# Mixer B's sample values on Trainium2: from two 64-column matmuls of 256 moving columns to four 32-column matmuls of 128

## The chip, the cores and the metric

The kernel runs on one core of a Trainium2 chip. The metric is the device time of one execution in microseconds (us), the median of several runs.

## What is computed

One step of a hybrid decoder layer over 1024 prompt rows and a group of 8 samples with 8 new tokens each. A projection of the inputs feeds two attention mixers, whose gated outputs go through a branch projection and an output projection with a layer norm. All data are float32. What the change touches is the attention of mixer B for the samples, over the cached keys and values of three head groups (window and dilation 128/1, 512/4, 2048/16); cut to that:

```python
def _gathered_attention(q, k, v, start, q_pos, dists, sink):
    ...
    s = jnp.einsum('nthgd,ntjhd->nthgj', q, kg).astype(jnp.float32) * SCALE
    p, lse = _masked_softmax(s, valid[None, :, None, None, :], sink)
    o = jnp.einsum('nthgj,ntjhd->nthgd', p.astype(v.dtype), vg)
    return o, lse
...
    for (win, dil), cache, q, k, v in zip(B_PAIRS, caches_b, qb, kb, vb):
        ...
        o, lse = _gathered_attention(q, kv[:, :, 0], kv[:, :, 1], PAST_LEN - cb, q_pos,
                                     np.arange(0, win + 1, dil), None)
        ...
    ob = _combine_dilations(outs, lses)
```

There are 4 key/value heads of 64 channels, 2 query heads to each, 8 samples and 8 new tokens.

## The kernel before

**The whole.** `in_proj` multiplies the weights by all rows, split into a high and a low part so that each product is three matmuls (L170, L171, L172, in chunks of 384, 384 and 320 moving columns). Weights come by DMA on the SP queue (`wraw<-w_in`), are rounded on ACT (`whi`, L89) and subtracted on DVE (`wlo`, L90). In its second part, `in_proj` makes the gates, and a generator, `beside()`, is advanced by a tick after every group of products: first the prompt's attention, then the samples' mixer A (`decode_a`), then the samples' mixer B (`decode_b`), then `merge`, which weighs and gates the attention outputs. Each tick lets the generator issue its next few instructions, so the program order on each engine is fixed when the kernel is built. Then come the branch projection (L1015 to L1017) and the output projection (L1058 to L1060).

**`decode_b`.** The samples go in four quads of two samples (`j` = 0, 1). For a quad, seven steps make the scores (L688, and L692 for the new keys), a softmax follows, and seven value steps add up the products of probabilities and values. Each of the 14 steps of a quad reads one tile `kv` (three buffers; loaded on POOL's queue two steps ahead, L661 for keys, L663 for values). 128 score rows stand on the partitions: 64 per sample, of which 32 belong to one pair of key/value heads (`kp` = 0, 1).

**A value step.** `transposes(gi + 1)` turns the probabilities of the next step (L726, copied to `pt` by ACT, L730). Then for each of the step's blocks of 128 keys (one in the first step, two in the other six) there are two matmuls (L746), one per sample: 64 columns of `pt` are the stationary operand, in half of the array's columns (`tile_position=(0, 64 * j)`), and 256 columns of `v`, all four heads, are the moving one. The first step adds the new tokens' values in the same way, with 24 rows (L741). All accumulate in one PSUM tile `acc` [128, 256].

**After the value steps.** DVE scales `acc` by the softmax's denominator (L751, into `o`), two steps of the generator later two transposes turn `o` (L756), and four copies on ACT (L762) take out, for each `kp`, the rows of `kp` in the columns of `kp`:

```python
pr = pa[:, :256].rearrange("d (k b q h g t) -> d k q h g b t", k=2, b=2, q=2, h=2, g=2)
...
        nc.scalar.copy(sr[r, kp, :, 2 * quad:2 * quad + 2], pr[r, kp, kp, h2])
```

The other half of `acc`, rows of one `kp` against columns of the other, is not read.

Of the kernel before, what the change touches and what calls it, by code (L numbers as in the profile page):

```python
# [10 lines left out]
F32 = mybir.dt.float32  # L11
# [3 lines left out]
ALU = mybir.AluOpType  # L15
# [4 lines left out]
P = 128  # L20
# [85 lines left out]
def layer_kernel(ctx: ExitStack, tc: tile.TileContext, A, O, S):  # L106
    nc = tc.nc
# [4 lines left out]
    ident = const.tile([P, P], F32, tag="ident", name="ident")  # L112
# [4 lines left out]
    def psd():  # L117
        return ps.tile([P, 512], F32, tag="d", name="psd")

    def psa():  # L120
        return ps.tile([P, 512], F32, tag="a", name="psa")
# [518 lines left out]
    def decode_b():  # L640
        with tc.tile_pool(name="db", bufs=1, side="right", reuse_waits="tile") as dp:
# [10 lines left out]
            def get(q, i):  # L652
                n = todo.index((q, i))
                for q_, i_ in todo[n:n + 3]:
                    if (q_, i_) not in tiles:
                        t = dp.tile([P, 2, 2, 256], F32, tag="kv", name="kv", bufs=3)
                        j, w = i_ % 7, COLS[i_ % 7]
                        for h in range(2):
                            if i_ < 7:
                                c = sum(COLS[:j])  # L660
                                nc.gpsimd.dma_start(out=t[:, h, :, :w], in_=A["ktb"][2 * q_ + h, :, :, c:c + w])  # L661
                            else:
                                nc.gpsimd.dma_start(out=t[:, h, :w // P], in_=A["vb"][2 * q_ + h, :, 2 * j - (j > 0):2 * j + 1])  # L663
                        tiles[q_, i_] = t
                return tiles[q, i]
# [4 lines left out]
            for quad in range(NB // 2):  # L670
                bs = (2 * quad, 2 * quad + 1)
                s = dp.tile([P, 1688], F32, tag="s", name="s")
                st = dp.tile([P, 16], F32, tag="st", name="st", bufs=2)
                vnew = dp.tile([24, 2, 256], F32, tag="vnew", name="vnew", bufs=1)
                for g in range(3):
                    for i in range(2):
                        nc.gpsimd.dma_start(
                            out=vnew[NQ * g:NQ * (g + 1), :, P * i:P * (i + 1)],
                            in_=S["sv"][1 + 2 * g + i, 16 * quad:16 * (quad + 1)].rearrange("(b t) c -> t b c", b=2))

                for ci in range(7):
                    cols, g = COLS[ci], (0, 1, 1, 2, 2, 2, 2)[ci]
                    pa = psa()
                    k = get(quad, ci)
                    for j, b in enumerate(bs):
                        for kp in range(2):
                            r = 64 * j + 32 * kp
                            nc.tensor.matmul(pa[r:r + 32, :cols], lhsT=qbd[:, g, b, kp], rhs=k[:, j, kp, :cols],  # L688
                                             start=True, stop=True, tile_position=(0, r))
                            if ci == 0:  # L690
                                for gg in range(3):
                                    nc.tensor.matmul(  # L692
                                        pa[r:r + 32, 128 + 8 * gg:136 + 8 * gg], lhsT=qbd[:, gg, b, kp],
                                        rhs=knew[:, gg, kp, NQ * b:NQ * (b + 1)], start=True, stop=True,
                                        tile_position=(0, r))
                    if ci == 0:
                        mm, sv, pv = mk[:, :152], s[:, :152], pa[:, :152]
                    elif g == 1:
                        lo = 152 + 256 * (ci - 1)
                        mm, sv, pv = mk[:, lo:lo + 256], s[:, lo:lo + 256], pa[:, :256]  # L700
                    else:
                        lo = 664 + 256 * (ci - 3)
                        mm = mk[:, 664 + 2 * (ci - 3):666 + 2 * (ci - 3)].unsqueeze(2).to_broadcast([P, 2, P])
                        sv = s[:, lo:lo + 256].rearrange("p (c k) -> p c k", c=2)
                        pv = pa[:, :256].rearrange("p (c k) -> p c k", c=2)
                    nc.vector.tensor_tensor(out=sv, in0=pv, in1=mm, op=ALU.add)
                    yield
                nc.vector.tensor_reduce(out=st[:, 0:1], in_=s, axis=AX.X, op=ALU.max)
                nc.vector.tensor_scalar(out=st[:, 1:2], in0=st[:, 0:1], scalar1=-0.125, scalar2=None, op0=ALU.mult)
                nc.scalar.activation(s, s, AF.Exp, bias=st[:, 1:2], scale=0.125, accum_out=st[:, 2:3])  # L710
                nc.vector.reciprocal(out=st[:, 3:4], in_=st[:, 2:3])
                yield
                yield
                yield
                acc = psa()
                starts = [0] + [152 + 128 * i for i in range(12)]
                ptn = dp.tile([24, P], F32, tag="ptn", name="ptn")
                ps_ = []

                def transposes(gi):  # L720
                    pa = psa()
                    p = dp.tile([P, 2, P], F32, tag="pt", name="pt", bufs=2)
                    w = COLS[gi] // P
                    for j in range(w):
                        c = starts[2 * gi - (gi > 0) + j]
                        nc.tensor.transpose(pa[:, P * j:P * (j + 1)], s[:, c:c + P], ident)  # L726
                    if gi == 0:
                        nc.tensor.transpose(pa[:24, P:2 * P], s[:, 128:152], ident)
                        nc.scalar.copy(ptn, pa[:24, P:2 * P])
                    nc.scalar.copy(p[:, :w], pa[:, :P * w].rearrange("p (b k) -> p b k", k=P))  # L730
                    ps_.append(p)

                transposes(0)
                yield
                for gi in range(7):
                    if gi < 6:
                        transposes(gi + 1)
                    p = ps_.pop(0)
                    if gi == 0:
                        for j in range(2):  # L740
                            nc.tensor.matmul(acc[64 * j:64 * (j + 1), :256], lhsT=ptn[:, 64 * j:64 * (j + 1)],  # L741
                                             rhs=vnew[:, j], start=True, stop=False, tile_position=(0, 64 * j))
                    v = get(quad, 7 + gi)
                    for jb in range(COLS[gi] // P):
                        for j in range(2):
                            nc.tensor.matmul(  # L746
                                acc[64 * j:64 * (j + 1), :256], lhsT=p[:, jb, 64 * j:64 * (j + 1)],
                                rhs=v[:, j, jb], start=False, stop=(gi == 6 and jb == 1), tile_position=(0, 64 * j))
                    yield
                o = dp.tile([P, 256], F32, tag="o", name="o")  # L750
                nc.vector.tensor_scalar(out=o, in0=acc[:, :256], scalar1=st[:, 3:4], scalar2=None, op0=ALU.mult)  # L751
                yield
                yield
                pa = psa()
                for kp in range(2):
                    nc.tensor.transpose(pa[:, P * kp:P * (kp + 1)], o[:, P * kp:P * (kp + 1)], ident)  # L756
                pr = pa[:, :256].rearrange("d (k b q h g t) -> d k q h g b t", k=2, b=2, q=2, h=2, g=2)
                sr = so.rearrange("d k g (b t) -> d k g b t", b=NB)
                for kp in range(2):
                    for h2 in range(2):  # L760
                        r = slice(HD * h2, HD * (h2 + 1))
                        nc.scalar.copy(sr[r, kp, :, 2 * quad:2 * quad + 2], pr[r, kp, kp, h2])  # L762
            for kp in range(2):
                for h2 in range(2):
                    nc.gpsimd.dma_start(out=S["num"][8 + 2 * kp + h2, :, NT:].rearrange("(g d) t -> d g t", g=2),
# [231 lines left out]
    gi = 78 * 4  # L997
    for part, (a, b) in enumerate(CHUNKS):
# [4 lines left out]
        for ft in range(KT):  # L1003
            ga, gb = nxt
            pa, pb = psd()[:, :n], psa()[:, :n]
            for j in range(3):
# [3 lines left out]
                o = pa if j < 2 else pb  # L1010
                for k4 in range(4):
                    k = 4 * j + k4
                    h, l = whi[:, k4 * P:(k4 + 1) * P], wlo[:, k4 * P:(k4 + 1) * P]
                    st, en = k in (0, 8), k in (7, 11)
# [19 lines left out]
        for i, (t, c) in enumerate(tiles):  # L1034
            h = hp.tile([P, DM], F32, tag=f"h{i}", name=f"h{i}")
# [43 lines left out]
        for nq in range(4):  # L1079
            pt = [psd() if i < 2 else psa() for i in range(len(tiles))]  # L1080
            if last and nq == 3:
                ws = []
                for i, (t, c) in enumerate(tiles):
# [8 lines left out]
                    h = hs[i][:c]  # L1092
                    v = mv[:c, 4 * i:4 * i + 4]
# [18 lines left out]
        if not last:  # L1112
            after(2, lambda: nc.scalar.activation(m4[:, :, 2], m4[:, :, 1], AF.Sqrt, bias=epst))
            nxt = load_g(0, *CHUNKS[part + 1])
            for i, (t, c) in enumerate(tiles):
                h, v = hs[i], mv[:, 4 * i:4 * i + 4]
# [133 lines left out]
```

## Time and profile before

| | |
|---|---|
| median of 3 runs | 2870.86 us (2870.16 to 2871.94) |
| the profiled execution's own time | 2865.24 us |
| its span, first to last instruction | 2863.5 us |
| PE (TensorE matmul) busy | 2760.6 us, 96% |
| DVE (VectorE) busy | 1530.0 us, 53% |
| ACT (ScalarE) busy | 925.8 us, 32% |
| POOL (GpSimd) busy | 770.9 us, 27% |
| mean granted TensorE clock | 0.983 of full speed |

PEld is TensorE's loading of the stationary operand. A float32 matmul instruction shows as two records (a high and a low pass), each with its own weight load; the text calls one record a pass. Matmul ends are modelled and overlap the next start, so the text takes times from one start to a later start. "Idle before" is an engine's idle time ahead of an instruction, with what ended it. The profiled execution is 5.6 us shorter than the median of the runs.

### The profile page before, as it was taken

The page shows a single profiled execution, that of the slowest core. Times are in us where ns is not written, and L with a number is a line of the kernel's source. Part 1 is how long each engine was busy: PE and PEld are TensorE (multiplying, and loading weights), DVE is VectorE, ACT ScalarE, POOL GpSimd, SP SyncE. Part 2 cuts the span into 40 slices and gives each one's busy share as a digit, 9 for nine tenths or more (in the row PEclk, how much of TensorE's full clock was granted, in tenths as well). Part 3 has the DMA queues.
Part 4 walks back from the last instruction along what each step waited for, and adds up shares of the span by engine and source line. Part 5 has one row for each costly group of instructions (what it writes and reads, how often), then busy time and mean ns, then how long its engine had stood idle before and what let it go on. Part 6 is the DMA issues. An engine that isn't in the chain of part 4 may idle for free.

```text
span 2863.5 us, 42950 instructions
## 1 busy us (share of the span) xinstructions
PE 2760.6 (96%) x16423; PEld 2641.7 (92%) x16423; DVE 1530.0 (53%) x2600; ACT 925.8 (32%) x1857; POOL 770.9 (27%) x589
## 2 busy tenths in 40 slices
PE   8999999999989999999999999999999996997898
PEld 8999999989989999999999998889899886986886
DVE  5444433423426778777665422116556458557856
ACT  4222222222223544444443321223144323432442
POOL 0000000000005666677677613432100025004201
PEclk9999999999999999999999999999999997998899
DMA  6345564465463333455445445559866535643662
GB/s 217 101 126 164 165 187 150 156 190 167 142 198 110 116 111 114 136 153 150 142 144 149 123 119 189 182 168 284 276 202 233 188 120 168 241 131 105 205 220 96
DMA packets 224965, 467.60 MB, mean 163 GB/s; under 512 B 33896, under 2 KB 151208, under 8 KB 221240
## 3 DMA queue, kind: packets, MB, share of 16 engines
q1 hardware_dynamic: 206264, 405.09, 45.0%
q0 software_dynamic: 16400, 52.43, 6.1%
q10 hardware_dynamic: 2096, 7.34, 0.7%
q8 instruction: 129, 2.11, 0.3%
q14 instruction: 76, 0.62, 0.1%
HBM read 365.17 MB, written 144.21 MB: 178 GB/s over the span
## 4 chain that ended last, share of the span: by engine, by line
PE 84%; DVE 6%; DMA 5%; SPq 2%; issue 1%; ACT 1%; POOL 0%; ACTq 0%; DVEq 0%; POOLq 0%
PE psd L170 19%; PE psd L172 18%; PE psd L171 18%; PE psd L1060 3%; PE psd L1059 3%; PE psd L1058 3%; PE psa L425 2%; PE psd L1017 2%; PE psd L1016 2%; PE psd L1015 2%; DMA wraw<-w_in 2%; DVE wlo L90 2%; SPq L321 1%; PE psa L487 1%; PE psa L486 1%
## 5 line engine op out<-in xcount | busy, mean ns | idle before, releaser
L170 PE MATMUL psd<-xhi,whi 128*128 128x384 f32 (+1 forms) x3712 | 1226.2, 330 | 26.4 <-ACT whi L89 23.8
L172 PE MATMUL psd<-xhi,wlo 128*128 128x384 f32 (+1 forms) x3712 | 1219.5, 329 | 2.1 <-DVE wlo L90 1.7
L171 PE MATMUL psd<-xlo,whi 128*128 128x384 f32 (+1 forms) x3712 | 1217.8, 328 | 0.3 <-DVE xlo L226 0.3
L90 DVE TENSOR_TENSOR wlo<-wraw,whi 128x512 fp32r<-128x512 f32 x648 | 482.2, 766 | 653.6 <-ACT whi L89 641.7
L170 PEld LDWEIGHTS psd<-xhi,whi 128*128 128x128 f32 x3712 | 699.9, 189 | 48.9 <-ACT whi L89 26.3
L172 PEld LDWEIGHTS psd<-xhi,wlo 128*128 128x128 f32 x3712 | 699.3, 188 | 5.7 <-DVE wlo L90 5.7
L171 PEld LDWEIGHTS psd<-xlo,whi 128*128 128x128 f32 x3712 | 699.7, 189 | 0.8 <-DVE xlo L226 0.8
L89 ACT CAST whi<-wraw 128x512 fp32r<-128x512 f32 x648 | 385.7, 618 | 592.2 <-DMA wraw<-w_in 348.8
L446 POOL PARTITION_ALL_REDUCE md<-s x160 | 214.6, 1341 | 1038.9 <-DMA vst<-s_vs 865.0
L460 POOL PARTITION_ALL_REDUCE md<-s x160 | 310.0, 1938 | 67.4 <-ACT s L457 44.2
L477 DVE TENSOR_TENSOR pl<-s,ph 128x512 fp32r<-128x512 f32 (+1 forms) x160 | 127.9, 800 | 100.4 <-ACT ph L476 98.4
L1017 PE MATMUL psd<-y,wlo 128*128 128x384 f32 (+1 forms) x384 | 129.1, 336 | 29.7 <-DVE wlo L90 29.7
L985 POOL TENSOR_TENSOR h<-h,mv 128x2048 f32<-128x2048 f32 x6 | 21.6, 3608 | 484.1 <-ACT whi L89 276.3
L1015 PE MATMUL psd<-y,whi 128*128 128x384 f32 (+1 forms) x384 | 129.1, 336 | 21.6 <-ACT whi L89 21.6
L1060 PE MATMUL psd<-wlo,m 128*128 128x512 f32 x384 | 149.8, 390 | 0.0
L1059 PE MATMUL psd<-whi,m 128*128 128x512 f32 x384 | 149.7, 390 | 0.0
L1058 PE MATMUL psd<-whi,m 128*128 128x512 f32 x384 | 149.6, 390 | 0.0
L457 ACT ACTIVATE s<-s 128x256 f32<-128x256 f32 (+1 forms) x160 | 75.9, 475 | 195.9 <-DVE s L456 193.8
L951 ACT ACTIVATE z<-psd,bias 128x384 f32<-128x384 f32 x132 | 73.8, 562 | 195.1 <-PE psd L172 129.4
L1016 PE MATMUL psd<-y,whi 128*128 128x384 f32 (+1 forms) x384 | 128.3, 334 | 0.0
L491 DVE TENSOR_TENSOR num<-psa,pvl 64x256 f32<-64x256 f32 x160 | 66.1, 413 | 77.3 <-ACT pvl L490 76.6
L1017 PEld LDWEIGHTS psd<-y,wlo 128*128 128x128 f32 x384 | 74.4, 194 | 32.1 <-DVE wlo L90 32.1
(202 smaller groups left out, 3183.4 us busy)
## 6 DMA issues: line engine op xcount, KB each, us to landing
wraw<-w_in SPq DMA_DIRECT2D x152, 512.0 KB
wraw<-w_out SPq DMA_DIRECT2D x96, 512.0 KB
wraw<-w_br SPq DMA_DIRECT2D x72, 512.0 KB
o_c<-c SPq DMA_DIRECT2D x64, 510.0 KB
qst<-s_qs SPq DMA_DIRECT2D x80, 256.0 KB
s_zg<-z SPq DMA_DIRECT2D x64, 192.0 KB
kv<-ktb POOLq DMA_DIRECT2D x48, 256.0 KB, 3.4
kv<-vb POOLq DMA_DIRECT2D x48, 256.0 KB, 3.1
```

The source lines that it names most:

```text
L89: self.nc.scalar.copy(hi, raw)
L90: self.nc.vector.tensor_tensor(out=lo, in0=raw, in1=hi.bitcast(F32), op=ALU.subtract)
L170: nc.tensor.matmul(o, lhsT=h, rhs=xhi[k][:, a:b], start=(k == 0), stop=False)
L171: nc.tensor.matmul(o, lhsT=h, rhs=xlo[k][:, a:b], start=False, stop=False)
L172: nc.tensor.matmul(o, lhsT=l, rhs=xhi[k][:, a:b], start=False, stop=(k == KT - 1))
L446: nc.gpsimd.partition_all_reduce(u["md"][:, 0], top, P, RED.max)
L460: nc.gpsimd.partition_all_reduce(u["md"][:, 1], s[:, 1 if n == 1 else 2], P, RED.add)
L1015: nc.tensor.matmul(o, lhsT=h, rhs=yt[k][:, 0, :n], start=st, stop=False)
L1017: nc.tensor.matmul(o, lhsT=l, rhs=yt[k][:, 0, :n], start=False, stop=en)
L1058: nc.tensor.matmul(pt, lhsT=h, rhs=whi, start=st, stop=False)
L1059: nc.tensor.matmul(pt, lhsT=l, rhs=whi, start=False, stop=False)
L1060: nc.tensor.matmul(pt, lhsT=h, rhs=wlo, start=False, stop=en)
```

## The change

The same products are made in quarters. For each block of 128 keys there are four matmuls in place of two, one per sample `j` and head pair `kp`: 32 columns of `pt` at array column `r = 64 * j + 32 * kp`, and only the 128 columns of `v` that belong to that `kp`. The new tokens' values go the same way. `acc` is used to 128 columns, `o` becomes [128, 128], one transpose takes the place of two, and the four copies read the smaller tile.

```diff
+                    ROWS = [(j, kp, 64 * j + 32 * kp) for j in range(2) for kp in range(2)]
                     if gi == 0:
-                        for j in range(2):
-                            nc.tensor.matmul(acc[64 * j:64 * (j + 1), :256], lhsT=ptn[:, 64 * j:64 * (j + 1)],
-                                             rhs=vnew[:, j], start=True, stop=False, tile_position=(0, 64 * j))
+                        for j, kp, r in ROWS:
+                            nc.tensor.matmul(acc[r:r + 32, :P], lhsT=ptn[:, r:r + 32],
+                                             rhs=vnew[:, j, P * kp:P * (kp + 1)], start=True, stop=False,
+                                             tile_position=(0, r))
                     v = get(quad, 7 + gi)
                     for jb in range(COLS[gi] // P):
-                        for j in range(2):
+                        for j, kp, r in ROWS:
                             nc.tensor.matmul(
-                                acc[64 * j:64 * (j + 1), :256], lhsT=p[:, jb, 64 * j:64 * (j + 1)],
-                                rhs=v[:, j, jb], start=False, stop=(gi == 6 and jb == 1), tile_position=(0, 64 * j))
+                                acc[r:r + 32, :P], lhsT=p[:, jb, r:r + 32],
+                                rhs=v[:, j, jb, P * kp:P * (kp + 1)], start=False, stop=(gi == 6 and jb == 1),
+                                tile_position=(0, r))
                     yield
-                o = dp.tile([P, 256], F32, tag="o", name="o")
-                nc.vector.tensor_scalar(out=o, in0=acc[:, :256], scalar1=st[:, 3:4], scalar2=None, op0=ALU.mult)
+                o = dp.tile([P, P], F32, tag="o", name="o")
+                nc.vector.tensor_scalar(out=o, in0=acc[:, :P], scalar1=st[:, 3:4], scalar2=None, op0=ALU.mult)
                 yield
                 yield
                 pa = psa()
-                for kp in range(2):
-                    nc.tensor.transpose(pa[:, P * kp:P * (kp + 1)], o[:, P * kp:P * (kp + 1)], ident)
-                pr = pa[:, :256].rearrange("d (k b q h g t) -> d k q h g b t", k=2, b=2, q=2, h=2, g=2)
+                nc.tensor.transpose(pa[:, :P], o, ident)
+                pr = pa[:, :P].rearrange("d (b q h g t) -> d q h g b t", b=2, q=2, h=2, g=2)
```

On PE, this is the difference of the two programs at the fourth and fifth value steps of the first quad, which stand directly behind each other (`s` are the probabilities, `ident` the identity of the transposes, `xhi_` and `xlo_` the parts of the layer's input):

```order
 L172 MATMUL psd<-xhi_155,wlo 128x384
 L726 MATMUL psa<-ident,s 128x128 x2
-L746 MATMUL psa<-kv,pt 64x256 x4
+L749 MATMUL psa<-kv,pt 32x128 x8
 L726 MATMUL psa<-ident,s 128x128 x2
-L746 MATMUL psa<-kv,pt 64x256 x4
+L749 MATMUL psa<-kv,pt 32x128 x8
 L170 MATMUL psd<-xhi_126,whi 128x384
```

The matmuls stand where they stood, twice as many, each of half the moving columns and half the array columns.

On POOL, this stands at the passage from `decode_b` to `merge`, with what each row waits for, before (`so` is the quad's output, `w`, `z` and `m` are merge's first tiles):

```order
471 L765 DMA s_num<-so 64x2x64 [waits DMASW3_49,Activation_49]
472 L841 DMA w<-s_wa 64x1024 [waits DMASW7_49,DMASW6_49,DMAHW2_49,DMASW4_49,PE_49]
473 L841 DMA w<-s_wa 64x1024 [waits DMASW5_49]
474 L844 DMA z<-s_z 128x1088 [waits DVE_49]
475 L798 DMA m<-s_md 32x1x256 [waits DVE_49,PE_49]
```

and this in the changed program:

```order
471 L768 DMA s_num<-so 64x2x64 [waits DMASW3_49,Activation_49]
472 L844 DMA w<-s_wa 64x1024 [waits DMASW5_49,DMAHW2_49,DMASW4_49,PE_49]
473 L844 DMA w<-s_wa 64x1024
474 L847 DMA z<-s_z 128x1088 [waits DMASW6_49,DMASW7_49,DVE_49,PE_49]
475 L801 DMA m<-s_md 32x1x256 [waits PE_49]
```

The order is the same; since `o` is smaller, merge's tiles lie over other tiles of `decode_b`, and the waits on its loads and on PE have moved between neighbouring rows.

## Rows read from the trace of the kernel before

**Rows 1.** The page: busy time, and the chain that ended last by engine.

```profile
PE 2760.6 (96%) x16423; PEld 2641.7 (92%) x16423; DVE 1530.0 (53%) x2600; ACT 925.8 (32%) x1857; POOL 770.9 (27%) x589
...
PE 84%; DVE 6%; DMA 5%; SPq 2%; issue 1%; ACT 1%; POOL 0%; ACTq 0%; DVEq 0%; POOLq 0%
```

**Rows 2.** Busy time by stretch: us, engines (instructions), granted clock, DMA share, GB/s.

```profile
1740.00:1760.00 20.00, 20.00 (x132) 15.12 (x129) 2.47 (x4) 3.04 (x8) 9.38 (x16) 1.00 0.65 205
1900.00:1920.00 20.00, 20.00 (x129) 17.05 (x128) 2.56 (x4) 5.17 (x13) 4.16 (x8) 1.00 0.26 84
1920.00:2080.00 160.00, 153.33 (x916) 152.21 (x916) 91.44 (x106) 41.22 (x68) 39.49 (x74) 0.99 0.91 280
```

**Rows 3.** Line L746: durations (ns min/median/max), first and last start (us), waits.

```profile
L746 PE MATMUL psa<-kv,pt x208: 378/379/432, 1740.2 to 1910.5; 128*64 128x256 f32 x104
...
  issue: 4.2, 24
  ACT pt L730: 1.2, 3
```

**Rows 4.** PE in order of time, a quad's first value steps: start, us, instruction, passes.

```profile
1739.30 0.38 PE L726 MATMUL psa<-ident,s 128*128 128x128 f32 x2
1739.61 0.65 PE L741 MATMUL psa<-vnew,ptn 24*64 24x256 f32 x4
1740.19 0.65 PE L746 MATMUL psa<-kv,pt 128*64 128x256 f32 x4
1740.77 0.45 PE L170 MATMUL psd<-xhi,whi 128*128 128x384 f32 x1
...
1743.30 1.08 PE L746 MATMUL psa<-kv,pt 128*64 128x256 f32 x8
1744.31 0.41 PE L170 MATMUL psd<-xhi,whi 128*128 128x320 f32 x1
```

**Rows 5.** PE in order of time, a score step with four 32-column matmuls.

```profile
1719.64 0.64 PE L688 MATMUL psa<-kv,qbd 128*32 128x256 f32 x8
1720.21 0.42 PE L170 MATMUL psd<-xhi,whi 128*128 128x320 f32 x1
```

**Rows 6.** The same, cut at 1719.80: the passes that had started by then.

```profile
1719.64 0.42 PE L688 MATMUL psa<-kv,qbd 128*32 128x256 f32 x4
```

**Rows 7.** Line L688 within 1719.6:1720.3: durations in ns, min/median/max.

```profile
L688 PE MATMUL psa<-kv,qbd x8: 378/391/404, 1719.6 to 1719.9; 128*32 128x256 f32 x8
```

**Rows 8.** A quad's first score step (lines L688, L692) as a stretch; columns as above.

```profile
1713.05:1714.48 1.43, 1.42 (x32) 1.41 (x32) 0.00 (x0) 0.00 (x0) 1.00 0.16 60
```

**Rows 9.** PE in order of time: the transposes of `o`, last quad.

```profile
1916.92 0.38 PE L756 MATMUL psa<-ident,o 128*128 128x128 f32 x2
1917.06 0.42 PE L170 MATMUL psd<-xhi,whi 128*128 128x384 f32 x1
```

**Rows 10.** POOL and ACT in order of time beside a quad's fourth and fifth value steps.

```profile
1751.40 1.06 POOL L663 DMA_DIRECT2D kv<-vb  x2 [2.46 <-PE psa L746]
...
1750.17 0.37 ACT L730 COPY pt<-psa 128x256 f32<-128x256 f32 x1 [2.63 <-PE psa L726]
```

**Rows 11.** Loads of values (L663): us from issue to landing.

```profile
DMA to landing us min/median/max: 2.3/3.1/5.5
```

**Rows 12.** PE in order of time: the fourth to last value steps of that quad.

```profile
1750.01 1.08 PE L746 MATMUL psa<-kv,pt 128*64 128x256 f32 x8
1751.02 0.44 PE L726 MATMUL psa<-ident,s 128*128 128x128 f32 x2
1751.39 1.09 PE L746 MATMUL psa<-kv,pt 128*64 128x256 f32 x8
...
1757.89 1.08 PE L746 MATMUL psa<-kv,pt 128*64 128x256 f32 x8
```

**Rows 13.** POOL and SP's queue in order of time at the start of merge.

```profile
1920.23 1.08 POOL L841 DMA_DIRECT2D w<-s_wa  x2
...
1921.80 0.32 SPq L838 DMA_DIRECT2D num<-s_num  x1
```

**Rows 14.** PE's only waits between 1920 and 2080 us, in order of time.

```profile
2017.09 0.44 PE L172 MATMUL psd<-xhi,wlo 128*128 128x384 f32 x1 [0.38 <-DVE wlo L90]
2027.46 0.69 PE L170 MATMUL psd<-xhi,whi 128*128 128x384 f32 x1 [4.53 <-ACT whi L89]
2044.96 0.44 PE L170 MATMUL psd<-xhi,whi 128*128 128x384 f32 x1 [1.76 <-ACT z L951]
```

More of the change, by code (lines that the diff above doesn't have):

```diff
@@ L761, in decode_b @@
                         r = slice(HD * h2, HD * (h2 + 1))
-                        nc.scalar.copy(sr[r, kp, :, 2 * quad:2 * quad + 2], pr[r, kp, kp, h2])
+                        nc.scalar.copy(sr[r, kp, :, 2 * quad:2 * quad + 2], pr[r, kp, h2])
             for kp in range(2):
```

## The prediction

> **What bounds the kernel now.** I began with the page's busy times and its chain of waits: PE is busy for 2760.6 us of a span of 2863.5 us, and 84% of the chain that ended last is PE's own work [rows 1]. A mean over stages does not tell what this stage is worth, so the next view is the table by stretch. `decode_b` runs from about 1700 to 1917 us. In a stretch of its value steps PE is busy for all of 20.00 us, at a granted clock of 1.00 (2.4 GHz), with DVE, ACT and POOL each busy for less than half of it and the DMA engines for 0.65 of it [rows 2]. The list of waits has no entry for PE from 1700 to 1920 us, and the waits that line L746 shows are the change of work on the engine itself ("issue", 24 times, 4.2 us) and three short ones on a copy of `pt` [rows 3]. So PE sets the pace here, and what it saves ends the stage earlier by as much, as long as nothing behind it takes the place.
>
> **The passes, as they run now.** L746 has 208 passes: in each of four quads one short burst of 4 and six long bursts of 8. L741 adds one burst of 4 per quad. From a burst's first start to the next instruction's start a long burst takes 1744.31 - 1743.30 = 1.01 us, a short one 1740.77 - 1740.19 = 0.58 us, and L741's 1740.19 - 1739.61 = 0.58 us [rows 4]. Passes run two beside each other, one in each half of the array, so a long burst has four rounds and a short one has two. Two rounds more cost 1.01 - 0.58 = 0.43 us, which makes a round of 256 moving columns 0.215 us, and the fixed part of a burst (filling at its start, emptying at its end) 0.58 - 0.43 = 0.15 us.
>
> **What the change does to a burst.** A long burst gets 16 passes of 128 columns in four array parts of 32. If the four run beside each other, it still has four rounds, but each of half the columns. Does this kernel run four such parts together? Its score steps do: four passes of 256 columns, the longest 404 ns [rows 7], start and end within 0.42 us [rows 6], and the whole burst of eight takes 1720.21 - 1719.64 = 0.57 us [rows 5]. That is eight passes of 256 columns in the time in which L746 does four of them [rows 4], with four different moving operands and one PSUM tile, as in the changed value steps. Four parts therefore cost no more time than two. A round of half the columns should take half of 0.215, that is 0.107 us. The steps are then:
>
> 1. Long bursts: 4 rounds of 0.107 + 0.15 = 0.58 us in place of 1.01, a gain of 0.43 us. There are 4 x 6 = 24, so 10.3 us.
> 2. Short bursts of L746: 2 x 0.107 + 0.15 = 0.37 in place of 0.58, a gain of 0.21. Four of them, 0.9 us.
> 3. L741's bursts, the same from 0.58: four, 0.9 us. It keeps its 24 rows, so there are as many changes between its shape and L746's as before.
> 4. One transpose of `o` in place of two. In the last quad the pair takes 1917.06 - 1916.92 = 0.14 us up to the next start, the second pass overlapping what follows [rows 9]. One pass of 128 columns less is 0.107 us, four times, 0.4 us.
>
> The sum is **12.5 us**. A weight load of 32 columns instead of 64 at the head of a burst may add a few hundredths to each of 32 bursts, so the upper end is 13.3 us.
>
> **What could eat part of it in the same stage.** The scaling on DVE and the four copies on ACT shrink or stay; PE meets their results two generator steps later, with whole groups of products between, so they are counted at nothing. The `pt` copies are tighter. Where two value steps stand directly behind each other, the second one's `pt` is ready at 1750.17 + 0.37 = 1750.54 [rows 10]; its burst starts at 1751.39 [rows 12] and would start at about 1750.96. That leaves 0.4 us, so the wait stays hidden. The `kv` loads are released by PE's bursts: the load of the last value step is issued at 1751.40 in two transfers that take POOL 1.06 us [rows 10], so the second leaves at about 1751.9, and lands 3.1 us later in the median and 5.5 at most [rows 11], at 1755.0 or at worst 1757.4. It is used at 1757.89 [rows 12], and after the change 0.9 us sooner counted from its release (two long bursts lie between). The cover is 2.0 us in the median; in the worst case 0.4 us is lost, in few of 28 steps, so 0 to 1 us. The waits that moved between rows of POOL and SP at merge's start ask for loads and PE work of `decode_b`, whose last transposes start at 1916.92 [rows 9], while those rows issue from 1920.23 and 1921.80 [rows 13]: nothing.
>
> **What comes behind.** From 1920 to 2080 us `merge` keeps the DMA engines 0.91 busy [rows 2], and PE waits three times, 0.38 + 4.53 + 1.76 = 6.7 us, for weights or a gate's copy [rows 14]. The gain must pass through this. Its transfers begin only behind `decode_b`'s last stores in program order, at 1920 us, and the 20 us ahead of it have the DMA engines at 0.26 [rows 2], so no queue is standing from before. I expect the whole stretch, its three waits included, to move ahead by the 12.5 us. Where transfers fall differently against the weights, I allow 1 us either way.
>
> **The rivals.**
>
> *The passes are bound by their issue.* Twice as many instructions make a burst denser: 16 passes in 0.58 us are one in 36 ns. The densest long run in this trace is a quad's first score step, 32 passes in 1.43 us, one in 45 ns [rows 8]. If that were a limit and not the chain of small matmuls on one array part that it is made of, a long burst would take 16 x 0.045 + 0.10 = 0.82 us and a short one 0.46: 24 x 0.19 + 8 x 0.12 + 0.4 = 5.9 us gained, 2865.0. Against it: the four passes that start within 0.02 us in rows 6. The Trainium skill, "TensorE: Matmul & The Clock Gate", section "Back-to-back issue gap", goes further and speaks against small passes: with hardware decoding off, the sequencer needs about 62 ns for each matmul; by that figure a long burst would be an estimated 16 x 0.062 + 0.10 = 1.09 us and the kernel about 2 us slower. The trace disagrees for runs of this length, with its 45 ns.
>
> *Merge gives it back.* If the transfers of 1920 to 2080 us, not PE, set that stretch's end, PE comes early and waits longer there. For it: a DMA share of 0.91 and the three waits. Lost between half and all of the gain: 2864.6 to 2870.9.
>
> *The parts don't overlap.* Slower, by one mechanism: in the value bursts passes of four 32-column parts run one behind another. A long burst would be 16 x 0.107 + 0.10 = 1.81 us, a short one 0.96: 24 x 0.80 + 8 x 0.38 - 0.4 = 21.8 us lost, 2892.7. It turns from gain to loss where a pass costs over (1.01 - 0.10) / 16 = 57 ns on average, that is where fewer than two run beside each other. Rows 5 and 6 speak against it; what they don't show is 128-column passes in four parts through several rounds. Two at a time, or for any other reason a pass every 57 ns, gives no change but the transposes' gain, about 2870.4.
>
> **How the numbers follow.** The profiled execution took 2865.24 us, 5.6 less than the median of the runs; the gain is a length of PE work, so I take it from the median: 2870.86 - 12.5 = 2858.4. Its own range is 2856 to 2861 (upper end of the sum, 1 us for `kv`, 1 us in merge either way). Chances: this forecast 0.77; issue-bound 0.06; merge gives back half or more 0.09; two at a time (or a pass every 57 ns) 0.04; one behind another 0.04. A measurement can tell about 0.2%, 5.7 us, from no change, so faster is below 2865.1: the forecast, most of the issue case and half of the merge case, 0.87; same 0.09; slower 0.04. The range from 2855.8 to 2865.0 takes in the forecast and the issue case and leaves about 0.16 out.
>
> **What would show it.** In the profile after: long bursts of 16 passes that take 0.55 to 0.60 us from first to next start, short ones 0.33 to 0.38, passes in fours within about 0.03 us; PE still without a wait up to `decode_b`'s end, which comes some 12.5 us earlier; the same three waits of PE in merge, about 6.7 us together. Long bursts of 0.8 us or more would show the issue case or worse; waits in merge that grew by the gain would show that rival. The forecast is wrong if the rounds are not halved by halving the columns.

## The result, and the profile after

The changed kernel took 2852.75 us (median of 4 runs, 2850.76 to 2854.97) beside 2870.51 us for the kernel before (median of 4 runs, 2867.98 to 2871.94): 17.8 us less, a ratio of 0.9939 with a 95% interval of 0.9922 to 0.9957. The direction was the one forecast, but 2852.75 lies below the range (2855.8 to 2865.0), and 17.8 us is more than the 12.5 us of the sum. In a second measurement, below, the same kernel came out 12.0 us faster. The question of the experiments is therefore which of the two is the change, and where the rest came from.

The profiled execution of the changed kernel took 2850.76 us. Its page, busy times and the chain by engine, answering to [rows 1]:

```profile
span 2849.0 us, 43393 instructions
PE 2749.8 (97%) x16643; PEld 2639.5 (93%) x16643; DVE 1530.5 (54%) x2600; ACT 925.9 (33%) x1857; POOL 770.9 (27%) x589
...
PE 85%; DVE 6%; DMA 3%; SPq 2%; issue 1%; ACT 1%; DVEq 0%; POOL 0%; ACTq 0%
```

PE lost 10.8 us of busy time. Its order of time in the first value steps answers to [rows 4]; L743 and L749 are the old L741 and L746, and the columns are start, us, instruction and passes:

```profile
1739.71 0.42 PE L743 MATMUL psa<-vnew,ptn 24*32 24x128 f32 x8
1740.06 0.43 PE L749 MATMUL psa<-kv,pt 128*32 128x128 f32 x8
1740.42 0.45 PE L170 MATMUL psd<-xhi,whi 128*128 128x384 f32 x1
...
1745.39 0.38 PE L726 MATMUL psa<-ident,s 128*128 128x128 f32 x2
1745.69 0.64 PE L749 MATMUL psa<-kv,pt 128*32 128x128 f32 x16
1746.27 0.44 PE L170 MATMUL psd<-xhi,whi 128*128 128x384 f32 x1
```

A long burst takes 1746.27 - 1745.69 = 0.58 us (1.01 before), a short one 1740.42 - 1740.06 = 0.36 and the new tokens' one 1740.06 - 1739.71 = 0.35 (0.58 each before). Cut at 1745.72, the same view shows that four passes had started within 0.03 us, and their ends lie within 0.32 us, as [rows 6] showed for the scores:

```profile
1745.69 0.32 PE L749 MATMUL psa<-kv,pt 128*32 128x128 f32 x4
```

What ended PE's idle times at L749, the answer to [rows 3], is the change of work on the engine and one short wait; the waits on `pt` are gone:

```profile
  issue: 4.8, 27
  ACT whi L89: 0.2, 1
```

Where the gain lies is seen from three places in program order, each with its first or last start in the trace: the first matmul on the new tokens' values, the last transpose of `o`, and the first matmul of the branch projection. Before:

```profile
L741 PE MATMUL psa<-vnew,ptn x16: 373/400/426, 1739.6 to 1891.9; 24*64 24x256 f32 x16
...
L756 PE MATMUL psa<-ident,o x8: 272/272/273, 1764.9 to 1917.0; 128*128 128x128 f32 x8
...
L1015 PE MATMUL psd<-y,whi x384: 307/336/689, 2114.5 to 2729.6; 128*128 128x384 f32 x128, 128*128 128x320 f32 x64
```

After:

```profile
L743 PE MATMUL psa<-vnew,ptn x32: 267/280/292, 1739.7 to 1882.6; 24*32 24x128 f32 x32
...
L759 PE MATMUL psa<-ident,o x4: 270/271/272, 1761.9 to 1904.8; 128*128 128x128 f32 x4
...
L1018 PE MATMUL psd<-y,whi x384: 307/336/687, 2098.1 to 2715.2; 128*128 128x384 f32 x128, 128*128 128x320 f32 x64
```

From the first place to the second it was 1917.0 - 1739.6 = 177.4 us and is 1904.8 - 1739.7 = 165.1: the value steps give **12.3 us**. (This stretch also holds the score steps of the last three quads, which the change leaves as they are.) From the second to the third, merge's stretch, it was 197.5 and is 193.3: 4.2 us more came from there. From the third to the end it is 1.9 us longer (749.0 and 750.9). The spans differ by 14.5 us; the rest up to 17.8 is that the profiled execution of the kernel before lies 5.3 us below its median, and that of the changed one 2.0 below. In merge's stretch PE's waits were 6.7 us [rows 14] and are 1.08 + 2.52 us in this execution, with a third of 0.2 us:

```profile
2011.09 0.45 PE L170 MATMUL psd<-xhi,whi 128*128 128x384 f32 x1 [1.08 <-ACT whi L89]
2028.21 0.44 PE L170 MATMUL psd<-xhi,whi 128*128 128x384 f32 x1 [2.52 <-ACT z L954]
```

### The profile page after: what moved, and what is told of

The parts are those of the page before. It is cut to its first block, busy times and chain, and to the rows that moved or that the text cites. A ratio compares the mean times of both kernels' runs of the same rounds, so it can differ in the third digit from the quotient of the medians.

```text
span 2849.0 us, 43393 instructions
## 1 busy us (share of the span) xinstructions
PE 2749.8 (97%) x16643; PEld 2639.5 (93%) x16643; DVE 1530.5 (54%) x2600; ACT 925.9 (33%) x1857; POOL 770.9 (27%) x589
## 4 chain that ended last, share of the span: by engine, by line
PE 85%; DVE 6%; DMA 3%; SPq 2%; issue 1%; ACT 1%; DVEq 0%; POOL 0%; ACTq 0%
PE psd L170 19%; PE psd L172 19%; PE psd L171 19%; PE psd L1063 3%; PE psd L1062 3%; PE psd L1061 3%; PE psa L425 2%; PE psd L1018 2%; PE psd L1019 2%; PE psd L1020 2%; DVE wlo L90 2%; SPq L321 1%; DMA wraw<-w_in 1%; PE psa L487 1%; PE psa L486 1%
```

## The experiments

Two theories stood at the start. **A:** the surplus over the 12.5 us is the change's too, through merge's stretch, either because merge's tiles now lie over others and their waits moved, or because PE arrives earlier. **B:** the surplus is the scatter of executions, and the change is worth its PE work.

### The changed kernel again, and with the old places of its tiles

> The changed kernel once more, in five rounds beside the kernel before. In the two profiles at hand PE's work up to 2016 us was 12.4 to 12.8 us shorter, and the rest of the measured 17.8 us (the medians) did not come from the value steps: 3.5 us of it is a wait of PE in merge that went from 4.53 to 1.1 us. Theory A (the extra is real, and of this kernel): about 17 us below the kernel before, 16 to 19. Theory B (the extra is the scatter of merge's transfers from one execution to the next): 12 to 14 us below.

```diff
-                o = dp.tile([P, P], F32, tag="o", name="o")
+                o = dp.tile([P, 256], F32, tag="o", name="o")[:, :P]
```

> The changed kernel with o allocated at its old size of 256 columns and used to 128, so that the tiles of decode_b and of merge lie where they lay before, and the waits at merge's start stand on the rows where they stood. PE does what it does in the changed kernel. If the extra gain behind decode_b comes from the moved tiles and waits: about 12.5 us below the kernel before. If it comes from anything else (an earlier arrival, or scatter): as the changed kernel in the same call, within 1.5 us.

Measured: the changed kernel 2855.86 us (6 runs, 2849.77 to 2859.27) and the one with the old places 2855.43 us (5 runs), beside 2867.4 us before (23 runs, 2862.17 to 2872.90). The ratios are 0.9958 (0.9946 to 0.9970) and 0.9956 (0.9944 to 0.9967), that is 12.0 and 12.6 us faster. The places of the tiles and the moved waits are worth nothing that shows. Theory B's number (12 to 14) came out, and theory A's first form falls; its second form, the earlier arrival, is taken up with merge below. The profiled execution of the repeat shows how far one program differs from itself: 2859.27 us where the first one took 2850.76.

```profile
L743 PE MATMUL psa<-vnew,ptn x32: 267/280/292, 1741.5 to 1884.1; 24*32 24x128 f32 x32
...
L759 PE MATMUL psa<-ident,o x4: 270/271/272, 1763.7 to 1906.2; 128*128 128x128 f32 x4
...
L1018 PE MATMUL psd<-y,whi x384: 307/336/687, 2108.2 to 2723.6; 128*128 128x384 f32 x128, 128*128 128x320 f32 x64
```

The value steps take 1906.2 - 1741.5 = 164.7 us, within 0.4 of the first execution. Merge's stretch takes 2108.2 - 1906.2 = 202.0 us, 8.7 more than in the other execution of the same program. Its waits are the same two, and longer:

```profile
2014.80 0.69 PE L170 MATMUL psd<-xhi,whi 128*128 128x384 f32 x1 [3.20 <-ACT whi L89]
2036.01 0.69 PE L170 MATMUL psd<-xhi,whi 128*128 128x384 f32 x1 [5.40 <-ACT z L954]
```

The first matmul behind each of them lasts 0.69 us, not the 0.45 and 0.44 of the other execution, because the granted clock had fallen: in the 4 us behind the second wait it was 0.50 (1.2 GHz), where the first execution, after a wait of 2.52 us, kept 1.00. Below, the repeat and then the first execution:

```profile
2036.01:2040.01 4.00, 4.00 (x12) 4.00 (x13) 2.22 (x3) 1.42 (x4) 1.02 (x2) 0.50 1.03 331
```

```profile
2028.21:2032.21 4.00, 4.00 (x25) 4.00 (x26) 2.21 (x3) 0.42 (x1) 1.02 (x2) 1.00 1.05 306
```

In its 4 us the repeat has 12 matmuls, the first execution 25. Of the 8.7 us, 4.8 are longer waits (8.6 us against 3.8); the lower clock behind them goes with the rest. Over the same 160 us of merge in either execution (us, engines, granted clock, DMA share, GB/s; first the first execution, then the repeat):

```profile
1908.00:2068.00 160.00, 156.29 (x943) 155.39 (x943) 95.75 (x112) 42.32 (x70) 39.20 (x73) 1.00 0.89 280
```

```profile
1908.00:2068.00 160.00, 151.40 (x889) 150.40 (x888) 89.59 (x105) 40.60 (x67) 40.68 (x76) 0.97 0.88 273
```

### The law of rounds

```diff
-                    for jb in range(COLS[gi] // P):
+                    w = COLS[gi] // P
+                    for n, jb in enumerate(2 * list(range(w))):
...
```

The new tokens' bursts are made twice in the same way, and `o` is halved.

> The changed kernel with every value burst made twice into the same sum, which is then halved: 32 passes of 128 columns in four parts, eight rounds, in place of 16 in four rounds. Tiles and waits lie as in the changed kernel. By the law of rounds a long burst takes 8 x 0.107 + 0.15 = 1.01 us, as before the change, a short one 0.58, so decode_b ends when it ended before the change, but for 0.4 us of transposes. If the extra gain comes from the moved tiles and waits: 4 to 5 us below the kernel before. If it comes from the earlier arrival or from scatter: 0 to 1 us below. If passes are bound by their issue (45 ns each) a long burst takes 1.54 us and the kernel is 15 us slower.

```diff
-                        for j in range(2):
+                        for j, kp, r in ROWS:
                             nc.tensor.matmul(
-                                acc[64 * j:64 * (j + 1), :256], lhsT=p[:, jb, 64 * j:64 * (j + 1)],
-                                rhs=v[:, j, jb], start=False, stop=(gi == 6 and jb == 1), tile_position=(0, 64 * j))
+                                acc[r:r + 32, :256], lhsT=p[:, jb, r:r + 32],
+                                rhs=v[:, j, jb], start=False, stop=(gi == 6 and jb == 1), tile_position=(0, r))
...
```

The new tokens' matmuls are split in the same way.

> The kernel before with four matmuls of 32 array columns in place of two of 64, but with all 256 moving columns: half of the change alone. Twice the passes, the same rounds. By the law of rounds a long burst stays at 1.01 us and the kernel at its time, within 1 us: the gain is in the halved columns, and the parts only allow it. If more parts cost by themselves (issue, operand reads), it is slower: at two at a time a long burst takes 1.87 us, 24 us in all. If the parts brought the gain, it is 12 us faster.

Measured: every burst made twice, 2864.67 us, ratio 0.9996 (0.9986 to 1.0005), no change. Four parts with all 256 columns, 2864.11 us, ratio 0.9988 (0.9979 to 0.9996), 3.4 us faster (1.1 to 6.0), which is more than the 1 us expected. PE's order of time, first with the bursts made twice, then with four parts of 256 columns:

```profile
1743.73 1.08 PE L750 MATMUL psa<-kv,pt 128*32 128x128 f32 x32
1744.74 0.42 PE L170 MATMUL psd<-xhi,whi 128*128 128x320 f32 x1
```

```profile
1742.32 1.07 PE L747 MATMUL psa<-kv,pt 128*32 128x256 f32 x16
1743.32 0.41 PE L170 MATMUL psd<-xhi,whi 128*128 128x320 f32 x1
```

Both long bursts take 1.00 to 1.01 us, as [rows 4] before the change: 32 passes of 128 columns, 16 passes of 256, or 8 passes of 256 in two parts. What counts is rounds times columns. In the value steps the parts by themselves bring nothing, the halved columns bring all. The value steps take 176.7 us (bursts twice, one transpose less) and 177.0 us (four parts) in these profiles, 177.4 before. So the 3.4 us of the second kernel don't come from its value steps; no experiment shows where from.

### The order of the passes

```diff
-                    for jb in range(COLS[gi] // P):
-                        for j, kp, r in ROWS:
+                    for j, kp, r in ROWS:
+                        for jb in range(COLS[gi] // P):
```

> The changed kernel with the two inner loops of a value step exchanged: all blocks of 128 keys of one array part, then the next part. The same 16 passes, in another order. If an instruction is handed to its array part as soon as that part's short queue has room, and parts run by themselves, a part begins some 30 to 60 ns after the one before it and a long burst takes 0.6 to 0.7 us in place of 0.57. If a part's passes must be done before the next part begins, it takes 4 x (0.134 + 3 x 0.109) + 0.1 = 1.95 us.

Measured: 2855.09 us (one run, with a profile). A long burst takes 0.60 us:

```profile
1742.41 0.66 PE L749 MATMUL psa<-kv,pt 128*32 128x128 f32 x16
1743.01 0.41 PE L170 MATMUL psd<-xhi,whi 128*128 128x320 f32 x1
```

Four passes that stand behind each other on one part hold up the next part hardly at all: 0.02 us a burst against the order by blocks. The next change takes the longer chains, in a quad's first score step:

```diff
-                    for j, b in enumerate(bs):
-                        for kp in range(2):
-                            r = 64 * j + 32 * kp
-                            nc.tensor.matmul(pa[r:r + 32, :cols], lhsT=qbd[:, g, b, kp], rhs=k[:, j, kp, :cols],
-                                             start=True, stop=True, tile_position=(0, r))
-                            if ci == 0:
-                                for gg in range(3):
...
+                    parts = [(j, b, kp, 64 * j + 32 * kp) for j, b in enumerate(bs) for kp in range(2)]
+                    for j, b, kp, r in parts:
+                        nc.tensor.matmul(pa[r:r + 32, :cols], lhsT=qbd[:, g, b, kp], rhs=k[:, j, kp, :cols],
+                                         start=True, stop=True, tile_position=(0, r))
+                    for gg in range(3 if ci == 0 else 0):
+                        for j, b, kp, r in parts:
...
```

> The changed kernel with a quad's first score step in the other order: the same 32 passes (one matmul on the keys and three of 8 columns on the new keys for each of four array parts), but going over the parts inside, so that neighbours in program order lie on different parts. Before, the chain on one part stood together, and the burst took 1.43 us, 45 ns a pass. If that was the chain on one part: 0.134 + 0.109 + 6 x 0.031 + 0.02 + 0.11 = 0.56 us, a gain of 0.87 us in four bursts, 3.5 us, ratio about 0.9946 where the changed kernel has 0.9958. If it was the limit at which passes can be issued (the rival of the prediction, 45 ns): it stays at 1.43 us.

> The changed kernel with a quad's first score step interleaved over the array parts, once more. PE's part of it is 3.6 us (the burst went from 1.43 to 0.52 us, four times). In four executions it came out 7.9 us below the changed kernel of another call. If the surplus is scatter of merge: 15 to 17 us below the kernel before. If it is of this kernel: 20 to 21 us.

Measured: 2846.02 us, ratio 0.9928 (0.9914 to 0.9943), in the first measurement, and 2848.75 us, ratio 0.9939 (0.9927 to 0.9952), in the second: 20.6 and 17.5 us faster than the kernel before. The burst:

```profile
1711.16 0.43 PE L687 MATMUL psa<-kv,qbd 128*32 128x128 f32 x8
1711.40 0.35 PE L691 MATMUL psa<-knew,qbd 128*32 128x8 f32 x24
1711.68 0.44 PE L170 MATMUL psd<-xhi,whi 128*128 128x384 f32 x1
```

The 32 passes take 1711.68 - 1711.16 = 0.52 us where they took 1.43 [rows 8]. The 24 small ones all start in this window, on average one in 7.5 ns (the window also holds the eight of L687 that still run):

```profile
1711.40:1711.58 0.18, 0.18 (x32) 0.18 (x24) 0.00 (x0) 0.00 (x0) 1.00 0.11 46
```

So the 45 ns a pass of [rows 8] came from the order, the chains on one array part, and were no limit of issue. The rival of the prediction falls with that. The gain by PE's work is 4 x 0.91 = 3.6 us on top of the change; the second measurement fits 12.4 + 3.6 within its interval, the first lies above it, so here too the first measurement was the larger. This kernel is faster than both.

### Merge's stretch

```diff
-                nc.sync.dma_start(out=num[:, :n], in_=S["num"][i + 4 * g, :, :n])
+                nc.gpsimd.dma_start(out=num[:, :n], in_=S["num"][i + 4 * g, :, :n])
```

> The changed kernel with merge's loads of num on POOL's queue in place of SP's, where they wait for a buffer ahead of weight loads and gate stores. Theory A (PE's waits in merge, and the scatter of that stretch from 168.7 to 177.4 us, come from SP's order): the waits of PE between 1905 and 2100 us fall from 3.8 to 8.6 us to under 1.5, the stretch to about 165 us, and the kernel is 16 to 20 us below the kernel before, with less scatter. Theory B (the transfers themselves are the limit there, the DMA engines are 0.91 busy): the waits stay within 3 to 9 us and the kernel within 2 us of the changed one.

> The kernel before with the same move of merge's num loads to POOL's queue. Its difference to num_pool is the change under study with merge's stretch altered in both in the same way. If the change is worth its PE work and nothing else, the two differ by 12.4 us, whatever the move does. If the earlier arrival in merge were worth something of its own, by 16 us or more.

Measured: 2871.16 us, ratio 1.0021 (1.0009 to 1.0033), and 2881.70 us, ratio 1.0052 (1.0037 to 1.0067). The move makes both kernels slower, by some 15 and 14 us. PE's waits in merge are 21.3 us with the change, where the changed kernel's two profiles have 3.8 and 8.6, and 17.7 without it, where the kernel before has 6.7. With the change:

```profile
PE psd L170 <- ACT z L954: 10.5, 2, 6.8
PE psd L172 <- DVE wlo L90: 7.7, 5, 4.4
PE psd L170 <- ACT whi L89: 3.1, 1, 3.1
```

Neither theory of that expectation holds: the waits neither fell nor stayed within 3 to 9 us. The move takes the loads out of SP's order and puts them into POOL's at once, so it doesn't show whether SP's order makes PE wait in the kernel as it stands, and no run shows why the move costs so much. Between each other the two differ by 10.5 us (medians), in executions that scatter over 18 us (2867.86 to 2885.79 with the change), so this says no more than that the change keeps its direction. The value steps differ by 177.4 - 165.1 = 12.3 us in these two profiles as well.

```diff
-            items = [(i, g) for i in range(12) for g in range(1 if i < 8 else 3)]
+            items = [(i, 0) for i in range(12)]
```

> The kernel before with a lighter merge: the second and third head group of mixer B are left out of the combination, so 8 of 20 loads of num and their weights fall away, with the DVE work on them; the sample's values for those groups are wrong. It takes the density out of the stretch behind decode_b. Theory A (the scatter from one execution to the next is that stretch's, where the single num buffer and the loads behind it make PE wait): 5 to 8 us below the kernel before, with executions within about 3 us of each other. Theory B (the scatter is in the turns of the clock, elsewhere): as scattered as before, 10 us from lowest to highest.

> The changed kernel with the same lighter merge. With the stretch behind decode_b no longer waiting, the change is worth its PE work: 12.0 to 12.8 us below light_b. If the change were worth more by arriving earlier in merge, that would vanish here and show as a difference to the 13 us between the full kernels; if 16 us or more remain, PE's own work was mis-sized.

Measured: 2863.28 us without the change (11 runs, 2859.57 to 2868.94), 2851.21 us with it (5 runs, 2845.81 to 2852.00), ratios 0.9989 (0.9980 to 0.9998) and 0.9942 (0.9929 to 0.9954). Both leave out the second and third head group of mixer B in `merge`. The change is worth 12.1 us between them by the medians, 13.6 by the means, which agrees with its PE work; the 16 us or more of the expectation did not come. But theory A about the scatter falls: without 8 of 20 loads, executions still lie 9.4 us apart. The waits of PE in merge are one kind each, 4.6 us without the change and 3.7 with it:

```profile
PE psd L170 <- ACT z L951: 4.6, 3, 2.6
```

```profile
PE psd L170 <- ACT z L954: 3.7, 1, 3.7
```

```diff
-RATES = (1.0, 1.15, 0.9)
+RATES = (1.0, 1.3, 0.79)
```

> The kernel of mix_again with other rates of the generator: 1.3 steps a tick in decode_a and decode_b (1.15), and 0.79 in merge (0.9), so that merge begins earlier and its transfers lie less densely. If PE's waits in merge come from that density: they fall from 4 to 9 us to under 2 us and the kernel is 3 to 5 us below mix_again, with less scatter. If denser value steps now wait for their kv loads, PE shows waits in decode_b and the gain is lost.

Measured, with the interleaved scores: 2850.89 us, ratio 0.9939 (0.9926 to 0.9951), the same as without the new rates. PE's waits in the profile are 2.4 + 1.8 us in merge, and 1.0 us that a score step waits for its `kv` load. The waits fell less than expected, and spreading merge out brought no gain.

### Where the scatter lies

The three places of the first section divide each profile into four stretches. In us, with the value steps in bold:

| kernel | to the first value matmul | value steps | merge's stretch | from the branch projection on | span |
|---|---|---|---|---|---|
| before | 1739.6 | **177.4** | 197.5 | 749.0 | 2863.5 |
| four parts, 256 columns | 1738.7 | **177.0** | 197.6 | 749.1 | 2862.4 |
| bursts made twice | 1740.1 | **176.7** | 198.7 | 747.4 | 2862.9 |
| before, lighter merge | 1741.4 | **177.3** | 195.6 | 747.2 | 2861.5 |
| changed | 1739.7 | **165.1** | 193.3 | 750.9 | 2849.0 |
| changed, again | 1741.5 | **164.7** | 202.0 | 749.3 | 2857.5 |
| changed, old places | 1741.7 | **165.0** | 195.6 | 751.3 | 2853.6 |
| changed, other order | 1739.2 | **165.4** | 200.8 | 747.9 | 2853.3 |
| changed, lighter merge | 1738.9 | **164.8** | 195.1 | 748.8 | 2847.6 |

The value steps repeat within 0.7 us on either side of the change. The stretch ahead of them, which the change doesn't touch, lies within 3.0 us, the last one within 4.1, merge's stretch within 8.7. With the full merge, merge's stretch takes 197.9 us on average over the first three kernels of the table, without the change's gain, and 197.9 over the four profiles that keep it; with the lighter merge it is 195.6 and 195.1. So, as far as these few profiles tell, merge hands the gain on and adds nothing that shows, and the 4.2 us of the first pair of profiles were luck. The stretches add up to the spans, so these are the places where profiled executions scatter. The kernel before, over 23, 17 and 15 runs of three later measurements, ranged from 2861.92 to 2874.13 us.

## Why the prediction was right and wrong

**What bounds the stage: right.** The list of PE's waits has no entry from 1700 us to `decode_b`'s end, before and after, and what PE saved shortened the stage by as much.

**The sum: right.** Steps 1 to 3 forecast bursts of 0.58, 0.37 and 0.37 us; they take 0.58, 0.36 and 0.35. Step 4 put a transpose at 0.11 us. In the last quad the next start came 0.14 us after the first of the pair [rows 9] and now comes 0.02 us after the only one, 0.12 less:

```profile
1904.76 0.27 PE L759 MATMUL psa<-ident,o 128*128 128x128 f32 x1
1904.78 0.43 PE L170 MATMUL psd<-xhi,whi 128*128 128x384 f32 x1
```

From the first value matmul to this start it was 1917.06 - 1739.61 = 177.45 us ([rows 4], [rows 9]) and is 1904.78 - 1739.71 = 165.07: 12.4 us, where the sum was 12.5. Six profiles of kernels that keep the change (those in the table, and the one with merge's loads on POOL's queue) give 164.7 to 165.4 us.

**What could eat part of it in the same stage: right.** L749 shows no wait for `kv` or `pt`, so the `kv` loads' cover held. The moved waits at merge's start cost nothing that shows: the changed kernel with the old places takes the same time within 0.5 us.

**What comes behind: the mechanism right, the size wrong.** Merge's stretch did move ahead by the gain, and no rival gave the gain back. But the term "1 us either way" for how transfers fall against the weights was far too small. The same program took 193.3 and 202.0 us there, and the first profile after had 4.2 us less than the one before. This is the term that was mis-sized: 1 us stood for what measures 8.7 us from one execution to another.

**How the numbers follow: the base and the range were wrong.** Apart from that 1 us, the prediction has no term for the scatter of executions. It subtracts the gain from the median of three runs that lie within 1.8 us (2870.16 to 2871.94), although the profiled execution, 2865.24 us, already stood 4.9 us below the lowest of them. Over 55 more runs the kernel before scatters over 12 us, with a mean of 2867.4. From there the sum gives 2867.4 - 12.5 = 2854.9 us; the mean of all 10 executions of the changed kernel is 2854.3. So most of the distance from the forecast, 2858.4, to the usual time of the changed kernel is the base, which stood 3.4 us too high.

The first result lies further off by chance on both sides, as far as the runs show. In the mean its four runs of the kernel before lie 2.8 us above the 55 later ones, and its four of the changed kernel 2.4 below the six of the repeat, and these two make the difference between 17.4 us and 12.2. The measured 17.8 us (12.3 to 22.4 by its interval) and the repeat's 12.0 (8.6 to 15.5) share 12.3 to 15.5 us. The later measurements ran on three chips, where the kernel before has means of 2867.6, 2867.3 and 2867.2 us; the chip of the first is not on record, so a difference between chips can't be ruled out. Over all 10 executions of the changed kernel and all 59 of the kernel before (2867.6), the difference is 13.3 us. What is shown is that the value steps are worth 12.3 us and that the rest of the first result lies in stretches that the same program runs through differently each time. That the change is worth nothing at all beyond its PE work is not shown: by an estimate from the scatter of these runs, 2 us more would not be seen. Why merge's stretch differs from one execution to the next stays open; lightening merge, spreading it out and moving its loads did not remove it.

**The rivals.** Issue: disproved, by long bursts of 0.58 us where that rival had 0.82, and by small passes that start 7.5 ns apart. Parts that don't overlap, or two at a time: disproved by the four passes that start within 0.03 us and by the same 0.58 us (1.81 and 1.01 there). Merge gives it back: disproved by merge's stretch, 197.9 us on average with and without the gain. The page of the Trainium skill, "TensorE: Matmul & The Clock Gate", section "Back-to-back issue gap", gives about 62 ns for each matmul where hardware decoding is off; the runs here, with 24 passes in 0.18 us, don't agree. No run shows whether hardware decoding was on.

## What to carry to other kernels

Where two heads' rows share a matmul and only the matching half of its columns is read, give each its own array part and its own columns: here a burst cost its rounds times the columns (0.107 us for a round of 128) plus a fixed 0.15 us, and four parts cost no more than two. Put passes that lie on different array parts next to each other in program order; a chain of eight on one part held up the parts behind it (1.43 us against 0.52 for the same 32 passes). And take the scatter of a kernel from many executions, stretch by stretch, before a range is stated: a stretch in which PE waits on late transfers can differ by more than the change is worth, while the stretch of the change itself repeats to a few tenths.

## What the runs showed that I had not expected

Small passes on four array parts start 7.5 ns apart on average, 24 in a row. Exchanging the loops, so that four passes of one part follow each other, cost only 0.02 us a burst, whereas eight passes on one part in a row, as in the old score step, cost 0.9 us. This would fit parts that are held up by the number of passes that stand ahead of them for one part; but the two bursts differ in the columns of their passes too, and no run shows from which number on it costs. And the loads of `num` moved from SP's queue to POOL's made the kernel 15 us slower.
